# The first expert's rows picked on TensorE, and a reordered router, in a hybrid encoder layer

## The chip, the cores and the metric

The kernel runs on one core of one Trainium2 chip. The metric is the device time of one execution in microseconds (us), less is better. Engines are named as the profile does: PE (TensorE), DVE (VectorE), ACT (ScalarE), POOL (GpSimd) and SP, which here only issues transfers.

## What is computed

One layer on 512 tokens of 1024 channels, all fp32: a mixer (a state-space group and an attention group beside each other, then an output projection), LayerNorm, a mixture of 16 experts in 4 groups, LayerNorm. The part at issue is the router and the way into the first expert:

```python
h = _layer_norm(ALPHA * h + mix, ln1_g, ln1_b)
g_logits = hf @ rg_w + rg_b                       # 4 groups
g_val, g_idx = lax.top_k(jax.nn.softmax(g_logits, axis=-1), 1)
e_logits = ...                                    # the 4 experts of the chosen group
e_val, e_idx = lax.top_k(jax.nn.softmax(e_logits, axis=-1), TOP_K)   # TOP_K = 2
e_val = e_val / jnp.sum(e_val, axis=-1, keepdims=True)
weights = g_val[:, None] * e_val
...
for e in range(N_EXPERTS):
    act = jax.nn.silu(hf @ w_gate[e]) * (hf @ w_up[e])
    out = out + combine[:, e:e + 1] * (act @ w_down[e])
h = _layer_norm(ALPHA * h + out, ln2_g, ln2_b)
```

## The kernel before

The 512 tokens are four tiles of 128, `hh[0]` to `hh[3]`, 128 tokens on the partitions by 1024 channels. A product that has to be close to fp32 is made as three products of split operands (a high part and a low part of each).

*Output projection.* A tile has two halves of 512 columns; the second pass over a half is 4 blocks of k with 3 products each (`pw`, L810). DVE adds the sum to `hh` (L816) and takes the half's statistics (L1289).

*LayerNorm 1, for each tile:* `norm_stats` (mean and variance; the power -1/2 on POOL, `rs`, L142 and L143), `norm_gain` on DVE (L1171), `norm_bias`: ACT scales by `rs` (L1177), POOL adds the bias (L1178). `norm_store` writes the tile to `hb` in DRAM (from which experts gather rows) and to `ub` (to which they add their results).

*Router.* `u_T` transposes `hh` before gain and norm (`phT`, L1195, ACT copies it to `hT`); `logits` is eight fp32 products for each tile (`plg`, L1200); DVE applies norm and bias to the 20 logits (`lg`, L1203). `choose` ranks them by comparisons (`d`, L1239 to L1242) and makes `og`, the chosen group, and `mskb`, the chosen experts, as 0/1 (L1243, L1244; both write into tiles that the trace calls `arena` and `mskb`). `seat` counts with ten products of 0/1 matrices the seat of each token within its expert (`ppos`, `place`, L1254). For an expert, `seats_of` makes four matrices `se` of 128 tokens by 128 seats (L937), and `list_of` multiplies them with `entry` (token number in two parts, weight in three parts) to the list of token numbers `ix` and weights `wc` (`plist`, L945). `gather` then reads the listed rows from `hb` (L958). `weigh` works out the weights of the two experts on DVE and writes them into `entry` (L1261 to L1283), with two exponentials on ACT.

*Experts.* `xg_T` transposes the gathered rows (`pxg`, L980) and splits them into `xgh` (ACT) and `xgl` (DVE); `gate_up` makes the products of gate and up (`pg`, `pu`, L1004 to L1006), `down` those back to 1024 channels. `wsplit` makes the high and low part of a piece of weights, `eh` on ACT and `el` on DVE (L987, L988). Pieces of weights (`raw`, 512 KB each) stream in on SP's queue, 30 of them ahead of the experts.

The order on PE is the program's order throughout. Within the router block the code stands under a manual schedule, so the order on DVE, ACT and POOL is the program's too. Before, expert 0's list is made first, its rows are gathered from DRAM, expert 1's list and gather follow, then `weigh`, the weights' parts of the two lists (`plist` with three columns), the count `pcnt` of tokens per expert, and then the transpositions and the first gate product.

## Time and profile before

| | us |
|---|---|
| median of 3 runs | 645.06 (644.91 to 646.80) |
| profiled execution | 646.35 |
| span of the profiled execution | 644.3 |
| PE busy in it | 577.7 (90%) |
| DVE busy | 529.4 (82%) |
| ACT busy | 415.0 (64%) |
| POOL busy | 252.7 (39%) |

The times inside the trace count from the start of the span, which is the profiled execution's own, 1.29 us above the median in time. Busy shares are means over stages that have different limits: projections, scan and attention up to some 285 us, the last output projections and the router up to some 322 us, the experts up to some 610 us, then the end. The stage that the change touches is the second of these.

### The profile page before, as it was taken

To read this page: it belongs to the slowest core of one execution; us is meant where nothing else is said; L and a number is where in the kernel's file an instruction comes from. 1 tells how busy PE (TensorE), PEld (TensorE's weight loads), DVE (VectorE), ACT (ScalarE), POOL (GpSimd) and SP (SyncE) were. 2 spreads that over 40 slices of the span, in tenths; PEclk is the share of its full clock that TensorE was granted. 3 is DMA by queue.
4 is the path that set the end of the run, shared out by engine and by line. 5 is a ranking of instruction groups with operands and counts; after the bars stand their busy time and mean duration, and the time that the engine had idled before them with its cause. 6 is when DMAs were issued, how large, how long until landed. Compare 5 with 4: busy or idle time off the path is not lost.

```text
span 644.3 us, 9107 instructions
## 1 busy us (share of the span) xinstructions
PE 577.7 (90%) x3007; PEld 476.5 (74%) x3007; DVE 529.4 (82%) x869; ACT 415.0 (64%) x629; POOL 252.7 (39%) x256
## 2 busy tenths in 40 slices
PE   6788996999999989999389999999999999999950
PEld 4577786988777758788278888888888888877830
DVE  4986789688668797675879999999999999999672
ACT  5444353543578775333277888888888888887670
POOL 6537623833453541026423322333333332211282
PEclk9997996999999999998599999999999999999985
DMA  7421222221222175985879999999999999991442
GB/s 267 136 72 58 65 66 66 83 65 52 80 67 65 34 243 193 388 338 187 318 282 307 322 373 358 373 358 356 344 340 358 361 351 353 336 340 45 126 168 84
DMA packets 61702, 141.39 MB, mean 219 GB/s; under 512 B 9987, under 2 KB 10003, under 8 KB 61648
## 3 DMA queue, kind: packets, MB, share of 16 engines
q1 hardware_dynamic: 55168, 125.79, 55.0%
q0 software_dynamic: 5904, 12.85, 7.1%
q10 hardware_dynamic: 576, 2.10, 0.8%
q8 instruction: 25, 0.41, 0.3%
q14 instruction: 29, 0.24, 0.1%
HBM read 134.69 MB, written 14.68 MB: 232 GB/s over the span
## 4 chain that ended last, share of the span: by engine, by line
PE 57%; DVE 15%; ACT 8%; DMA 7%; issue 6%; POOL 5%; SPq 0%; POOLq 0%; ACTq 0%; DVEq 0%
PE pw L810 6%; PE pg L1004 5%; PE pg L1006 4%; PE pg L1005 4%; PE py L1038 4%; PE pu L1004 4%; PE pu L1006 4%; PE pu L1005 4%; PE py L1040 4%; PE py L1039 4%; PE pjT L250 3%; DVE acc L437 3%; DMA wr<-in_wu 2%; PE pxg L980 2%; POOL wl L234 1%
## 5 line engine op out<-in xcount | busy, mean ns | idle before, releaser
L987 ACT ACTIVATE eh<-wf 128x1024 fp32r<-128x1024 f32 x192 | 203.1, 1061 | 49.8 <-PE pg L1006 15.0
L234 POOL TENSOR_TENSOR wl<-wr,wh 128x512 fp32r<-128x512 f32 x40 | 56.8, 1441 | 43.5 <-ACT wh L229 40.7
L958 POOL DMA_INDIRECT xg<-hb,ix x16 | 21.0, 1315 | 113.1 <-PE pg L1006 107.9
L1044 POOL DMA_INDIRECT ub<-yo,ix x15 | 27.4, 1829 | 88.5 <-ACT at L103 54.4
L1038 PE MATMUL py<-eh,at 128*128 128x512 f32 x128 | 52.4, 410 | 2.7 <-ACT at L103 2.5
L1004 PE MATMUL pg<-eh,xgh 128*128 128x512 f32 x128 | 53.1, 415 | 0.8 <-ACT xgh L103 0.8
L1040 PE MATMUL py<-eh,at 128*128 128x512 f32 x128 | 50.9, 398 | 0.0
L1006 PE MATMUL pg<-eh,xgl 128*128 128x512 f32 x128 | 50.7, 396 | 0.0
L1004 PE MATMUL pu<-eh,xgh 128*128 128x512 f32 x128 | 50.0, 391 | 0.0
L1006 PE MATMUL pu<-eh,xgl 128*128 128x512 f32 x128 | 49.9, 390 | 0.0
L274 PE MATMUL pjR<-wh,xh 128*128 128x256 f32 x128 | 39.8, 311 | 8.9 <-ACT acc L429 7.5
L250 PE MATMUL pjT<-xh,wh 128*128 128x512 f32 x112 | 46.3, 413 | 1.2 <-DVE kl L674 1.2
L250 PE MATMUL pjT<-xh,wl 128*128 128x512 f32 x112 | 44.1, 394 | 0.0
L250 PE MATMUL pjT<-xl,wh 128*128 128x512 f32 x112 | 44.0, 393 | 0.0
L937 POOL TENSOR_SCALAR se<-seats,place 128x128 bf16<-128x128 f32 x56 | 43.4, 790 | 0.5
L274 PE MATMUL pjR<-wl,xh 128*128 128x256 f32 x128 | 38.3, 299 | 0.0
L274 PE MATMUL pjR<-wh,xl 128*128 128x256 f32 x128 | 38.1, 298 | 0.0
L274 PEld LDWEIGHTS pjR<-wh,xh 128*128 128x128 f32 x128 | 26.9, 210 | 9.6 <-ACT acc L429 7.9
L1038 PEld LDWEIGHTS py<-eh,at 128*128 128x128 f32 x128 | 24.5, 191 | 8.5 <-ACT at L103 2.7
L1040 PEld LDWEIGHTS py<-eh,at 128*128 128x128 f32 x128 | 24.4, 191 | 5.9 <-DVE at L104 0.8
L1006 PEld LDWEIGHTS pg<-eh,xgl 128*128 128x128 f32 x128 | 24.3, 190 | 6.0 <-DVE xgl L104 0.7
L1004 PEld LDWEIGHTS pg<-eh,xgh 128*128 128x128 f32 x128 | 24.3, 190 | 5.0 <-ACT xgh L103 1.2
(952 smaller groups left out, 1759.6 us busy)
## 6 DMA issues: line engine op xcount, KB each, us to landing
wf<-in_w_up SPq DMA_DIRECT2D x64, 512.0 KB, 11.6
wf<-in_w_gate SPq DMA_DIRECT2D x64, 512.0 KB, 11.7
wf<-in_w_down SPq DMA_DIRECT2D x60, 512.0 KB, 12.2
wr<-in_wu SPq DMA_DIRECT2D x22, 512.0 KB, 3.9
wor<-in_w_out SPq DMA_DIRECT2D x8, 512.0 KB, 3.3
hh<-in_x SPq DMA_DIRECT2D x4, 512.0 KB, 5.2
wf<-in_w_down POOLq DMA_DIRECT2D x4, 512.0 KB, 7.3
u<-ub SPq DMA_DIRECT2D x4, 512.0 KB, 6.0
```

The source lines that it names most:

```text
L234: G.tensor_tensor(l_[:, j], wr_[:, j], h_[:, j].bitcast(F32), op=OP.subtract)
L250: T.matmul(pt, lhsT=w_[:, k % 4, m * P:(m + 1) * P], rhs=x_[k], start=(i == 0), stop=(i == 23))
L274: T.matmul(pt, lhsT=x_[k][:, t * P:(t + 1) * P], rhs=w_[:, k % 4, :], start=(i == 0), stop=(i == 23))
L810: T.matmul(pw, lhsT=m_[k][:, ts_], rhs=wo[k][w_][:, c_], start=(i == 0), stop=(i == 11))
L937: eng.tensor_scalar(r[t], seats, place_(t), None, op0=OP.is_equal)
L987: A.activation(h_, src, AF.Copy)
L1004: T.matmul(pt, lhsT=h_[:, k], rhs=wh_[:, f], start=(k == 0), stop=False)
L1005: T.matmul(pt, lhsT=h_[:, k], rhs=wl_[:, f], start=False, stop=False)
L1006: T.matmul(pt, lhsT=l_[:, k], rhs=wh_[:, f], start=False, stop=(k == KC - 1))
L1038: T.matmul(pt, lhsT=h_[:, f], rhs=wh_[:, c_], start=(f == 0), stop=False)
L1040: T.matmul(pt, lhsT=l_[:, f], rhs=wh_[:, c_], start=False, stop=(f == 3))
L1044: G.indirect_dma_start(out=ub, out_offset=bass.IndirectOffsetOnAxis(ap=ix, axis=0), in_=yo, in_offset=None, bounds_check=S - 1, oob_is_err ...
```

## The change

Tiles 0 and 1 are chosen and seated while tile 2 is still projected (`choose(0, 2)`, `seat(0, 2)`), tiles 2 and 3 behind the logits. The rows of expert 0 are no longer gathered from DRAM and transposed: for each tile DVE makes a 0/1 matrix `pick[t]` (token by seat, in the memory of expert 0's `xg` tile), and PE multiplies `hh[t]`, 128 channels at a time, with it, summed over the four tiles. What results, `px`, is already transposed (channel by seat). A product of zeros opens each of its two banks; 32 products of 128x128 fp32 follow, the eight of tile 0 ahead of `seat(2, 4)`. `weigh` is cut in two by a `yield`, its first half ahead of the split of `px`, its second half behind it; then comes expert 0's list as a whole, then expert 1's weights and the count. Tile 2's bias is done by DVE in one operation (`NBV`), all stores go by POOL's queue, expert 1's matrices are made on POOL, and `og` is made with an added factor of ones.

```diff
-NBV = ()
+NBV = (2,)
-NXG = 26
+NXG = 25
-        se = seats_of(lp, lambda t: place[:, t, e:e + 1], V if e < 2 else G)
+        se = seats_of(lp, lambda t: place[:, t, e:e + 1], G)
...
-        V.tensor_scalar(c["og"], c["rank"][:, :, 0], 0.0, None, op0=OP.is_equal)
+        V.scalar_tensor_tensor(c["og"], c["rank"][:, :, 0], 0.0, onesf[:, None].to_broadcast([P, n, 4]), op0=OP.is_equal,
+                               op1=OP.mult)
...
+        for t in range(t0, t1):
+            pick[t] = xgs[0][:, t * P:(t + 1) * P]
+            V.scalar_tensor_tensor(pick[t], seats, place[:, t, 0:1], onesf.to_broadcast([P, P]), op0=OP.is_equal, op1=OP.mult)
+
+    def picked(ts, ks):
+
+        for k in ks:
+            if k % 4 == 0 and len(px) == k // 4:
+                px.append(bank("pj", "px"))
+
+                T.matmul(px[-1], lhsT=identb, rhs=maskq[:, 0:1].to_broadcast([P, 512]), start=True, stop=False)
+            for t in ts:
+                T.matmul(px[k // 4][:, k % 4 * P:(k % 4 + 1) * P], lhsT=hh[t][:, k * P:(k + 1) * P], rhs=pick[t],
+                         start=False, stop=(t == NT - 1 and k % 4 == 3))
...
                 if t == 2:
                     logits(1)
+                    choose(0, 2)
+                    next(ph_)
+                    next(ph_)
+                    next(ph_)
+                    seat(0, 2)
                 drop(ph_)
...
-        logits(2, range(4))
+        logits(2, range(3))
+        u_T(3, 1)
         logits(3, range(4))
         norm_stats(3)
-        norm_store(2, hb, A)
-        u_T(3, 1)
+        norm_store(2, hb, G)
         norm_gain(3)
...
         norm_shift(3)
...
+        norm_bias(3)
         logits(3, range(4, 8))
...
-        choose(2, 4)
-        seat()
-        call(0, False)
...
-        call(1, False)
-        load_pieces(NPRE, NPRE + GATED, G)
-        weigh()
-        for e in range(2):
-            lists[e][1] = list_of(lp, lists[e][1], entry_of(e), tokens=False)[1]
-        for i in range(2, 4):
-            dsp[0, i] = wsplit(raw[0, i])
+        logits(2, range(3, 8))
+        choose(2, 4)
+        picked((0,), range(KC))
+        seat(2, 4)
+        norm_store(3, hb, G)
+        picked((1,), range(KC))
+        picked((2, 3), range(4))
+        dsp[0, 2] = wsplit(raw[0, 2])
+        wg_ = weigh()
+        next(wg_)
+        xt_ = [wide("x", n, NX).rearrange("p (k s) -> p k s", s=P) for n in ("xgh", "xgl")]
+        for hf in range(2):
+            if hf:
+                picked((2, 3), range(4, 8))
+            split(*(t_[:, hf * 4:hf * 4 + 4] for t_ in xt_), px[hf].rearrange("p (k s) -> p k s", s=P))
+        call(1, False)
+        for t in range(2, 4):
+            norm_store(t, ub, G)
+        load_pieces(NPRE, NPRE + GATED, G)
+        dsp[0, 3] = wsplit(raw[0, 3])
+        drop(wg_)
+        lists[0] = list_of(lp, seats_of(lp, lambda t: place[:, t, 0:1], V), entry_of(0))
+        lists[1][1] = list_of(lp, lists[1][1], entry_of(1), tokens=False)[1]
-    xt_ = xg_T(xgs[0])
```

*First place: PE, from the last logits to the seats and from there to the first gate.* In the kernel before, the logits of tile 2 and of tile 3 are followed by the seat products, and the end of the stretch is the count (`pcnt`, a product of 0/1 matrices), the transpositions of the gathered rows (`pxg`) and the gate:

```order
L1358 LDWEIGHTS onesb
L1358 MATMUL pcnt<-mskb,onesb 128x16
L980 MATMUL pxg<-identf,xg_3007 128x128 x8
L1004 MATMUL pg<-eh,xgh 128x512
L1005 MATMUL pg<-el__3041,xgh 128x512
L1006 MATMUL pg<-eh,xgl 128x512
```

In the changed kernel the picks of tile 0 (`px`, with `hh` as the operand held in PE, and `xg_3005`, the memory of the 0/1 matrices, as the other) stand between the logits and the seat products:

```order
L1195 MATMUL plg_3019<-gw,hT 128x20 x3
L1190 MATMUL phT<-identf,hh 128x128 x4
L1195 MATMUL plg_3020<-gw,hT 128x20 x8
L1195 MATMUL plg_3019<-gw,hT 128x20 x5
L1264 LDWEIGHTS identb
L1264 MATMUL px<-maskq,identb 128x512
L1266 MATMUL px<-xg_3005,hh 128x128 x4
```

(the last three rows come once more, for the second bank) and the other 24 stand between the seat products (`ppos`) and the lists (`plist`, `se` the 0/1 matrices of an expert):

```order
L1251 MATMUL ppos<-mskb,onesb 128x16
L1252 LDWEIGHTS strictb
L1252 MATMUL ppos<-mskb,strictb 128x16
L1266 MATMUL px<-xg_3005,hh 128x128 x24
L940 LDWEIGHTS se
L940 MATMUL plist<-entry,se 128x2
```

and the gate follows the count directly:

```order
L1379 LDWEIGHTS onesb
L1379 MATMUL pcnt<-mskb,onesb 128x16
L999 MATMUL pg<-eh,xgh 128x512
L1000 MATMUL pg<-el__3041,xgh 128x512
L1001 MATMUL pg<-eh,xgl 128x512
```

The eight transpositions have gone from the place ahead of the gate; 32 products and two products of zeros have come, 24 of the products between the seats and the lists.

*Second place: DVE, behind the choice of tiles 2 and 3 (`mskb`).* In the kernel before, the place of each token (`place`) is followed by expert 0's matrices and list:

```order
L1243 TENSOR_SCALAR arena_3292<-arena_3292 128x8
L1244 SCALAR_TENSOR_TENSOR mskb<-arena_3292 128x32
L1254 SCALAR_TENSOR_TENSOR place<-ppos,mskb 128x64
L937 TENSOR_SCALAR se<-seats,place 128x128 x4
L950 TENSOR_REDUCE if__3336<-plist 128x1
L951 TENSOR_SCALAR ix<-if__3336 128x1
```

In the changed kernel by two picks, a low half of weights (`el`), the first half of `weigh`, and the split of `px`:

```order
L1253 SCALAR_TENSOR_TENSOR place<-ppos,mskb 128x32
L1256 SCALAR_TENSOR_TENSOR xg_3005<-seats,place,onesf 128x128 x2
L983 TENSOR_TENSOR el__3357<-wf,eh 128x1024
L1274 TENSOR_REDUCE arena_3180<-lg_3021 128x20
L1275 TENSOR_TENSOR lg_3021<-lg_3021,arena_3180 128x80
L1279 SCALAR_TENSOR_TENSOR arena_3360<-arena_3180 128x64
L1282 TENSOR_TENSOR arena_3360<-arena_3360,lg_3021 128x64
L1284 TENSOR_REDUCE arena_3180<-arena_3360 128x4
L1279 SCALAR_TENSOR_TENSOR arena_3180<-arena_3180 128x64
L99 TENSOR_TENSOR xgl<-px,xgh 128x512 x2
L945 TENSOR_REDUCE if__3394<-plist 128x1
L946 TENSOR_SCALAR ix<-if__3394 128x1
```

The split of the rows has moved ahead of the second half of `weigh`, and expert 0's matrices (L937, now L932) have left this place.

*Third place: DVE, at the end of the router.* In the kernel before, the last weights (`entry`) are followed by the weights' lists and by the low halves:

```order
L1283 TENSOR_TENSOR arena_3292<-arena_3292,entry 128x64
L1281 CAST entry<-arena_3292 128x64
L954 TENSOR_REDUCE wc<-plist 128x1 x2
L988 TENSOR_TENSOR el__3399<-wf,eh 128x1024
L988 TENSOR_TENSOR el__3403<-wf,eh 128x1024
L1359 TENSOR_REDUCE cnt_i<-pcnt 128x1
```

In the changed kernel by expert 0's four matrices and its whole list:

```order
L1297 TENSOR_TENSOR arena_3180<-arena_3180,entry 128x64
L1295 CAST entry<-arena_3180 128x64
L932 TENSOR_SCALAR se<-seats,place 128x128 x4
L945 TENSOR_REDUCE if__3433<-plist 128x1
L946 TENSOR_SCALAR ix<-if__3433 128x1
L949 TENSOR_REDUCE wc<-plist 128x1 x2
L1380 TENSOR_REDUCE cnt_i<-pcnt 128x1
```

The matrices and the list of expert 0 stand between the last of `entry` and the count, where there were only the weights' lists.

## Rows read from the trace of the kernel before

**Rows 1.** Busy time by stretch; columns: stretch, its us, PE, PEld, DVE, ACT, POOL, PEclk, DMA, GB/s

```profile
313.50:321.78 8.28, 2.48 (x22) 2.07 (x22) 6.86 (x26) 2.91 (x5) 5.70 (x8) 0.50 0.88 289
337.00:480.00 143.00, 142.69 (x700) 117.32 (x701) 137.10 (x169) 119.01 (x143) 50.19 (x50) 1.00 0.99 347
```

**Rows 2.** Chain of waits over the router; columns: start us, us, what

```profile
313.55 6.39 DMA xg<-hb,ix
...
319.98 1.97 PE pxg L980 x8
```

**Rows 3.** Timeline of PE; columns: start us, us, engine, line, operation, [idle before <-releaser]

```profile
292.24 1.05 PE L810 MATMUL pw<-woh,m 128*128 128x512 f32 x2
...
300.84 1.89 PE L1200 MATMUL plg<-gw,hT 128*128 128x20 f32 x16
...
304.63 1.89 PE L1200 MATMUL plg<-gw,hT 128*128 128x20 f32 x8 [0.62 <-ACT hT L1196]
...
318.86 0.25 PE L1358 MATMUL pcnt<-mskb,onesb 128*128 128x16 bf16 x4
...
321.78 0.80 PE L1004 MATMUL pg<-eh,xgh 128*128 128x512 f32 x1
...
324.51 0.45 PE L1004 MATMUL pu<-eh,xgh 128*128 128x512 f32 x1
```

**Rows 4.** Timeline of DVE, router

```profile
289.69 0.24 DVE L1203 SCALAR_TENSOR_TENSOR lg<-plg,rs,sh 128x20 f32<-128x20 f32 x1 [0.20 <-PE plg L1200]
...
303.25 1.39 DVE L1171 SCALAR_TENSOR_TENSOR hh<-hh,mv,l1g 128x1024 f32<-128x1024 f32 x1 [0.36 <-PE phT L1195]
...
305.80 0.33 DVE L1241 TENSOR_TENSOR d<-d,ahead 128x160 f32<-128x160 f32 x1
...
306.52 2.17 DVE L1243 TENSOR_SCALAR arena<-arena 128x8 f32<-128x8 f32 x1
...
308.83 0.23 DVE L1203 SCALAR_TENSOR_TENSOR lg<-plg,rs,sh 128x20 f32<-128x20 f32 x1
...
310.17 0.17 DVE L1243 TENSOR_SCALAR arena<-arena 128x8 f32<-128x8 f32 x1
310.37 0.19 DVE L1244 SCALAR_TENSOR_TENSOR mskb<-arena 128x32 bf16<-128x32 f32 x1
...
311.19 0.87 DVE L937 TENSOR_SCALAR se<-seats,place 128x128 bf16<-128x128 f32 x4
...
314.02 0.23 DVE L1261 TENSOR_REDUCE arena<-lg 128x20 f32<-128x80 f32 x1
...
315.22 0.16 DVE L1273 TENSOR_REDUCE arena<-arena 128x4 f32<-128x16 f32 x1
...
318.34 0.26 DVE L1281 CAST entry<-arena 128x64 bf16<-128x64 f32 x1
...
319.11 1.30 DVE L988 TENSOR_TENSOR el__3399<-wf,eh 128x1024 fp32r<-128x1024 f32 x1
...
322.62 0.69 DVE L104 TENSOR_TENSOR xgl<-pxg,xgh 128x512 fp32r<-128x512 f32 x1 [0.16 <-ACT xgh L103]
```

**Rows 5.** Timeline of PE, late in the program

```profile
609.32 2.05 PE L1114 MATMUL pl<-l2in,identf 16*128 16x128 f32 x16
```

**Rows 6.** Timeline of POOL, router

```profile
290.81 2.36 POOL L1178 TENSOR_TENSOR hh<-hh,l1b 128x1024 f32<-128x1024 f32 x1 [2.83 <-ACT hh L1177]
...
303.52 1.54 POOL L143 TENSOR_TENSOR rs<-rs,mhalf 128x1 f32<-128x1 f32 x1
306.32 2.34 POOL L1178 TENSOR_TENSOR hh<-hh,l1b 128x1024 f32<-128x1024 f32 x1 [1.26 <-ACT hh L1177]
```

**Rows 7.** Timeline of POOL, early in the program

```profile
43.15 6.32 POOL L234 TENSOR_TENSOR wl<-wr,wh 128x512 fp32r<-128x512 f32 x4 [12.51 <-ACT wh L229]
```

**Rows 8.** Timeline of DVE, in the same stretch

```profile
45.31 1.23 DVE L438 TENSOR_TENSOR acc<-acc,lack 128x3 f32<-128x3 f32 x1
```

**Rows 9.** Timeline of ACT, router

```profile
321.98 0.60 ACT L103 ACTIVATE xgh<-pxg 128x512 fp32r<-128x512 f32 x1 [0.26 <-PE pxg L980]
```

More of the change, by code (lines that the diff above doesn't have):

```diff
@@ L48 @@
 EARLY = 3
-NBV = ()
-NBO = 0
-CHO = 1
-UB = "AA"
+NBV = (2,)
 PT = ("o", "s")
 RY = 1.0
-HBE = 1
-UBE = 1
-NXG = 26
+NXG = 25
 WH_P = (0, 1)
@@ L1242, in choose, with seat @@
         V.tensor_reduce(rows_(c["rank"]), d, axis=AX.X, op=OP.add)
-        V.tensor_scalar(c["og"], c["rank"][:, :, 0], 0.0, None, op0=OP.is_equal)
+        V.scalar_tensor_tensor(c["og"], c["rank"][:, :, 0], 0.0, onesf[:, None].to_broadcast([P, n, 4]), op0=OP.is_equal,
+                               op1=OP.mult)
         V.scalar_tensor_tensor(mskb[:, t0:t1].rearrange("p t (g e) -> p t g e", e=4), c["rank"][:, :, 1:5], 2.0,
                                c["og"][:, :, :, None].to_broadcast([P, n, 4, 4]), op0=OP.is_lt, op1=OP.mult)
-    def seat():
+    pick, px = {}, []
+    def seat(t0, t1):
         pp_ = bank("s", "ppos")[:, :64].rearrange("p (t e) -> p t e", e=16)
-        for t in range(NT):
+        for t in range(t0, t1):
             for tt in range(t):
@@ L1253, in seat @@
             T.matmul(pp_[:, t], lhsT=strictb, rhs=mskb[:, t], start=(t == 0), stop=True)
-        V.scalar_tensor_tensor(place, pp_, 1.0, mskb, op0=OP.add, op1=OP.mult)
+        V.scalar_tensor_tensor(place[:, t0:t1], pp_[:, t0:t1], 1.0, mskb[:, t0:t1], op0=OP.add, op1=OP.mult)
+        for t in range(t0, t1):
+            pick[t] = xgs[0][:, t * P:(t + 1) * P]
[8 more added lines that the diff above has]
+                         start=False, stop=(t == NT - 1 and k % 4 == 3))
     def weigh():
@@ L1272, in weigh @@
                 A.activation(r1, r1, AF.Exp)
+        yield
         V.tensor_reduce(gs, gx, axis=AX.X, op=OP.add)
@@ L1292, in hybrid_layer @@
         for t in range(NT):
-            drop(proj_half(t, 0))
+            ph_ = proj_half(t, 0)
+            if t == 3:
+                next(ph_)
+                next(ph_)
+                u_T(2, 0)
+                u_T(2, 1)
+                norm_gain(2)
+            drop(ph_)
             if t in DSP0:
@@ L1297, in hybrid_layer @@
                 norm_shift(t - 1)
-                u_T(t - 1, 0)
-                u_T(t - 1, 1)
-                norm_gain(t - 1)
+                if t < 3:
+                    u_T(t - 1, 0)
+                    u_T(t - 1, 1)
+                    norm_gain(t - 1)
                 norm_bias(t - 1)
@@ L1305, in hybrid_layer @@
                     logits(1)
+                    choose(0, 2)
+                    next(ph_)
+                    next(ph_)
+                    next(ph_)
+                    seat(0, 2)
                 drop(ph_)
@@ L1309, in hybrid_layer @@
                     logits(0)
-                if t == 2 and CHO == 0:
-                    choose(0, 2)
                 if t:
-                    norm_store(t - 1, hb, (A, G)[HBE])
-                    norm_store(t - 1, ub, (A, G)[UBE])
+                    norm_store(t - 1, hb, G)
+                    norm_store(t - 1, ub, G)
         next(ph_)
@@ L1318, in hybrid_layer @@
         drop(ph_)
[L1319 removed]
+        logits(2, range(3))
+        u_T(3, 1)
         logits(3, range(4))
         norm_stats(3)
[L1322 to L1323 removed]
+        norm_store(2, hb, G)
         norm_gain(3)
[L1325 to L1327 removed]
         norm_shift(3)
[L1329 to L1356 removed]
+        norm_bias(3)
+        logits(3, range(4, 8))
+        logits(2, range(3, 8))
[14 more added lines that the diff above has]
+        call(1, False)
+        for t in range(2, 4):
+            norm_store(t, ub, G)
+        load_pieces(NPRE, NPRE + GATED, G)
+        dsp[0, 3] = wsplit(raw[0, 3])
+        drop(wg_)
+        lists[0] = list_of(lp, seats_of(lp, lambda t: place[:, t, 0:1], V), entry_of(0))
+        lists[1][1] = list_of(lp, lists[1][1], entry_of(1), tokens=False)[1]
+    pn = bank("s", "pcnt")[:, :16]
     for tt in range(NT):
@@ L1367, in hybrid_layer @@
         if e < NEXP - 2:
-            gu = gate_up(e, xt_)
+            gu = gate_up(e, xt_, "pj" if e else "o")
             for _ in range(EARLY):
```

18 lines of the change are left out of this document (removed).

## The prediction, made before the changed kernel had run

> **What bounds the kernel now.** Read first is the busy time by stretch [rows 1]. From 337 to 480 us, where the experts run, PE is busy 142.69 of 143.00 us at a granted clock of 1.00 (2.4 GHz): nothing there is to be had by shortening a wait. From 313.50 to 321.78 it is busy 2.48 of 8.28 us, at 0.50 (1.2 GHz). So the router, between the last row product of the output projection and the first gate product of expert 0 (321.78, [rows 3]), is a hole in PE's work, and what the change does to the time is what it does to the start of that product. The experts behind it move as one block: the same products follow in the same order, and PE has no slack to give or take.
>
> Second comes the chain of waits over the hole [rows 2]. Its largest piece is the gather of expert 0's rows, 6.39 us from 313.55; then the eight transpositions, 1.97 us, and the gate. What the chain does not show stands in DVE's list [rows 4]: while the gather flies, DVE works out the weights of the chosen experts (from 314.02 to 318.60) and makes two low halves of weights (from 319.11). The gather ends at 319.94, the weights' lists and the count at 319.1 (the `pcnt` row, 318.86 and 0.25). The gather thus hides the weighing nearly to the end. That is the question to ask of a change that takes the gather away: what is late next?
>
> **What goes.** For expert 0: the gather (6.39), its eight transpositions (1.97), and ahead of them the four 0/1 matrices and the list (seats and all, 3.0 us from `mskb`'s end at 310.56 to the gather at 313.55). Earlier choosing of tiles 0 and 1 also takes 1.73 us of DVE (`lg` to `mskb`, 308.83 to 310.56 where nothing stalls, [rows 4]) and the stall of 2.17 us in it out of tile 3's way. If nothing came in their place the gate could begin some 11 us sooner; all of it does get a substitute.
>
> **What comes, step by step, on the clock of the trace.**
>
> (a) *Tile 2.* The 0/1 choice of tiles 0 and 1 now follows `lg` at 289.69, and three seat products stand on PE after nine of the twelve products of tile 2's second half. The choice runs into POOL's bias add, 290.81 to 293.17 [rows 6]. The trace has the same pair: `og`, 8 elements wide, normally 0.17 us, took 2.17 us in 306.52 to 308.69 beside the add of 306.32 to 308.66 [rows 4, 6]. That the new `og` is an operation with two inputs is no way out: a two-input operation of 3 elements took 1.23 us beside POOL's subtractions [rows 7, 8]. So `mskb` comes at about 293.17 + 0.2 + 0.2 = 293.6, while the ninth product ends near 292.7 (the pair that begins at 292.24 is the ninth and tenth, two in 1.05, [rows 3]). PE and all behind it wait 1.0 us (bounds 0 and 2.0).
> The Trainium skill (SBUF — State Buffer, section SBUF: two separate sides) says that the port pair of the two engines is an exclusive lock for a whole instruction, which a DVE operation takes in a two-port mode or with two SBUF inputs; the 2.17 and 1.23 us agree with it. By it the rewritten `og` waits as the old one did, and the sum is the one given here; were it free of it, (a) would be 0 and the second stall in (c) nothing.
>
> (b) *Tile 3's norm.* `rs` ended at 303.52 + 1.54 = 305.06, held by DVE's gain of 303.25 to 304.64 [rows 4, 6]. The gain now waits for a transposition that stands 0.36 us earlier. With (a): 305.06 - 0.36 + 1.0 = 305.7.
>
> (c) *The choice of tiles 2 and 3.* After `rs` DVE does the shift, two `lg` and the comparisons; the second comparison would begin at about rs + 1.1 (0.74 in the trace, 305.80, plus two `lg` of under 0.2), POOL's add at rs + 1.26 (306.32), for 2.34. So `og` is caught, the comparison at the edge of it. With both caught, `mskb` is at rs + 1.26 + 2.34 + 0.3 + 0.35 + 0.2 + 0.2 = rs + 4.7 = 310.4; with none of it and without (a), at 304.7 + 2.4 = 307.1. Before it was 310.56. I take 310.4, since the trace shows this very collision.
>
> (d) *PE ahead of the seats.* From 302.0 on PE has 16 logit products, four transpositions, two zero products that open the banks, and the eight products of tile 0. The trace has two records for each fp32 product, so a logit product costs 1.89 / 8 = 0.24 at full clock, 1.89 / 4 = 0.47 at half clock (300.84 and 304.63, [rows 3]). At full clock it is through at 308.7, under the cover of (c); the ten seat products come right behind `mskb` and end at 310.7. Without (c)'s stall it would end at 307.6, just about with `mskb`.
>
> (e) *The remaining 24 products* of 128x128 fp32 by a 128x128 0/1 matrix. The trace has none; the nearest row has fp32 products of 128 columns, 2.05 / 8 = 0.25 us each at full clock, though with 16 partitions [rows 5]; the other bound is the half-clock 0.47. PE has by then stood some 2 us, and in the trace, after standing, it ran at half clock from 321.78 to 324.51, 2.7 us, before a product took 0.45 instead of 0.80 [rows 3]. At full clock throughout: 24 x 0.25 = 6.0, end 316.7. Restarting at half clock: 5.8 products in 2.7 us, 18.2 in 4.6, end 318.0. I take the middle, 317.3. Other DVE work (two picks, one low half of 1.3, the first half of the weighing, 1.2) fits under it.
> The Trainium skill (Perfetto Trace Analysis, section Transposes) asks for a transposition rather than an ordinary product where data are only moved. Here the eight transpositions took 1.97 us at half clock (0.25 each), the product at that clock 0.47, which agrees; and there are 32 products for 8 transpositions. By that rule the change should lose on PE, and the sum says so too.
>
> (f) *DVE's tail behind the last product.* Now nothing flies that could hide it. In its new order: ACT's high half 0.65 [rows 9] and DVE's low half 0.16 + 0.69; the list of expert 1, two operations, 0.35; a low half of weights 1.25; the second half of the weighing, 315.22 to 318.60, 3.38 less a wait, 3.25; four matrices 0.87; then lists, weights and count, 1.2, an estimate: from `entry`'s end at 318.60 to `pcnt`'s end at 319.11 it took 0.5 for two hand-overs between DVE and PE, and here there are four and three short operations [rows 3, 4]. Sum 8.4. The first gate stands behind the lists and the count in PE's order, so it starts at 317.3 + 8.4 = 325.7, against 321.78: +3.9 us.
>
> Edits that I cost at nothing: expert 1's matrices on POOL, which is idle from about 310 (needed only an expert later); the moved stores and the piece of weights that now waits for them (its reader is three experts on); one preload fewer ahead; gate banks "o" (their last readers, the logits, are long done). If the cover of expert 1's gather (expert 0's 48 gate and up products) were gone, it would cost its 6.39.
>
> **Sum.** The profiled execution took 646.35 us (span 644.3), 1.29 above the median of the three runs, 645.06. 646.35 + 3.9 = 650.3 on its clock, 649.0 against the median. A measurement of this kernel can tell about 0.3%, 1.9 us, from no change.
>
> **The rivals.**
> 1. *It comes out even.* No collision on DVE in (a) and (c), full clock: seats at 307.9, last product 313.9, gate 322.3, +0.5, 645.6 us. For it: the second `og` of the trace took 0.17; the two queues shift by tenths of a microsecond. Against: the add's start hangs on the same `rs` as the choice.
> 2. *Faster.* A product by a 0/1 matrix costs about what a transposition costs at full clock, half of 0.25. With 24 x 0.12 and no collision DVE's chain alone is left: 307.1 + 11.9 = 319.0, -2.8, 642.3 us. It decides where a product costs under about 0.15 and nothing collides. Against: the logit products, with a sixth of the columns, cost 0.24.
> 3. *Much slower.* PE never comes back to 2.4 GHz in the hole, as in the 8.28 us ahead of the gate in the trace [rows 1]: 24 x 0.47 = 11.3 behind 310.7, gate 330.4, +8.6, 653.7 us; with the logits at half clock too, 657.9.
>
> **How the numbers follow.** Main case (DVE's weighing is what is late next, +2 to +6 us): 0.58. Even: 0.23. Faster: 0.09. Much slower: 0.10. The likeliest gives 649.0. The range leaves out the faster case and most of the much slower one: 644.4 (the even case, 1.2 below its 645.6) to 654.5. The main case's own range is 647.0 to 651.5. Faster by over 0.3%: 0.09; within: 0.24; slower: 0.67.
>
> **What would show it.** Right: the chain of waits has no gather between `mskb` and the first gate; PE waits for DVE's `entry` or `se`, and the first gate begins near 325.7; the 24 `px` products take 6 to 7.5 us together; an `og` of about 2 us beside POOL's add. Wrong: a gate before 322, the last `px` product before 314, or a hole behind the first gate that was not there before, as expert 1's rows or a piece of weights arriving late would make.

## The result, and the profile after

The changed kernel takes 649.87 us in the median of 4 runs (649.08 to 650.59), against 645.6 us of the kernel before measured beside it (644.91 to 646.80): ratio 1.0071, interval 1.0055 to 1.0086. It is slower by 4.3 us, and the prediction had said 649.0, +3.9 on its own trace. The profiled execution took 650.47 us, span 648.5.

The busy time by stretch of the kernel after (columns as in [rows 1]: stretch, its us, PE, PEld, DVE, ACT, POOL, PEclk, DMA, GB/s) has the hole in another place:

```profile
302.40:312.00 9.60, 9.31 (x63) 8.93 (x61) 6.84 (x14) 3.23 (x4) 6.22 (x6) 0.69 0.86 307
312.00:318.00 6.00, 6.00 (x55) 5.92 (x52) 3.85 (x11) 1.03 (x4) 2.28 (x2) 0.93 0.59 203
318.00:325.40 7.40, 0.87 (x12) 0.59 (x11) 6.06 (x24) 1.53 (x2) 5.51 (x8) 0.84 0.43 157
325.40:330.10 4.70, 4.70 (x15) 3.71 (x16) 0.78 (x2) 1.06 (x1) 1.10 (x2) 0.52 1.01 384
```

From 302.40 to 318 PE is busy nearly throughout, with logits and picks, where before it stood. From 318 to 325.4 it is busy 0.87 of 7.40 us. In these 7.4 us the second half of the weighing is done and expert 0's matrices and list are made. Before, the weighing ran while the gather flew, and the matrices and the list stood ahead of the gather. Then the gate runs 4.7 us at a granted clock of 0.52.

The chain of waits names the pieces (start us, us, what):

```profile
292.17 2.18 DVE arena L1238
...
294.61 0.17 PE ppos L1252
...
307.62 0.43 PE px L1264
308.05 1.71 PE px L1266 x8
...
310.18 1.71 PE px L1266 x8
...
312.06 5.91 PE px L1266 x48
...
318.48 1.06 ACT eh L982
...
319.56 1.23 DVE el__3407 L983
...
322.04 0.56 DVE entry L1295
...
325.33 0.28 PE pcnt L1379 x4
325.61 0.63 PE pg L999
```

No gather and no transposition of gathered rows stands in it any more [rows 2]: it goes from `og` beside POOL's add (292.17) through the picks (`px`) to the two halves of a piece of weights (`eh` on ACT, 318.48, and `el` on DVE, 319.56), the weighing (`entry`, 322.04), the count (325.33), and the gate.

PE's timeline of the kernel after (as [rows 3]) shows the three waits of PE that the change made or moved, and the price of a pick:

```profile
294.61 0.17 PE L1252 MATMUL ppos<-mskb,strictb 128*128 128x16 bf16 x1 [1.62 <-DVE mskb L1240]
...
303.41 0.63 PE L1190 MATMUL phT<-identf,hh 128*128 128x128 f32 x4 [0.29 <-DVE hh L811]
...
311.91 6.04 PE L1266 MATMUL px<-xg,hh 128*128 128x128 f32 x48
...
324.11 0.82 PE L940 MATMUL plist<-entry,se 128*128 128x5 bf16 x8 [6.08 <-DVE se L932]
325.33 0.28 PE L1379 MATMUL pcnt<-mskb,onesb 128*128 128x16 bf16 x4 [0.40 <-DVE wc L949]
325.46 0.77 PE L999 MATMUL pg<-eh,xgh 128*128 128x512 f32 x1
```

The 24 picks behind the seats took 6.04 us with the last one's modelled end, 5.91 in the chain: 0.25 each, at a clock of 0.93 from 312 to 318. Then PE waited 6.08 us for `se` and 0.40 for the list's weights, and the first gate product began at 325.46.

DVE's timeline (as [rows 4]) has both stalls beside POOL's adds:

```profile
292.17 2.17 DVE L1238 SCALAR_TENSOR_TENSOR arena<-arena,onesf 128x8 f32<-128x8 f32 x1
...
307.93 1.91 DVE L1234 TENSOR_TENSOR d<-lg 128x160 f32<-128x160 f32 x1
309.88 0.33 DVE L1236 TENSOR_TENSOR d<-d,ahead 128x160 f32<-128x160 f32 x1
...
310.59 0.17 DVE L1238 SCALAR_TENSOR_TENSOR arena<-arena,onesf 128x8 f32<-128x8 f32 x1
310.79 0.30 DVE L1240 SCALAR_TENSOR_TENSOR mskb<-arena 128x32 bf16<-128x32 f32 x1
...
316.83 0.69 DVE L99 TENSOR_TENSOR xgl<-px,xgh 128x512 fp32r<-128x512 f32 x1 [1.44 <-ACT xgh L98]
318.62 0.69 DVE L99 TENSOR_TENSOR xgl<-px,xgh 128x512 fp32r<-128x512 f32 x1 [1.10 <-ACT xgh L98]
```

and POOL's (as [rows 6]) the adds:

```profile
291.95 2.35 POOL L1173 TENSOR_TENSOR hh<-hh,l1b 128x1024 f32<-128x1024 f32 x1 [1.72 <-ACT hh L1172]
...
307.32 2.35 POOL L1173 TENSOR_TENSOR hh<-hh,l1b 128x1024 f32<-128x1024 f32 x1 [0.73 <-ACT hh L1172]
```

The new `og` took 2.17 us, as the old one did; the two-input form is no way out. At the second place it was the first comparison that was caught (1.91 us), and `og` then ran in 0.17. The two idle times ahead of `xgl` (in the brackets: 1.44 and 1.10 us of DVE waiting for the picked rows) are the ones in which the first experiment puts the weighing.

**How the trace of the prediction stands among others of the same kernel.** Two more traces of the kernel before were taken later. The stages count here from the first transposition of tile 0 (`phT`), so that differences in the first stages fall out; each column is the start of one event, in us behind it. The last column is the measured time against before.

| kernel | last projection product | last seat product | first gate product | expert 1's transpositions | time |
|---|---|---|---|---|---|
| before, the trace of the prediction | 22.5 | 32.7 | 43.7 | 56.3 | |
| before, second trace | 21.0 | 31.1 | 41.9 | 54.4 | |
| before, third trace | 21.0 | 31.1 | 41.4 | 54.5 | |
| after | 22.9 | 32.7 | 46.3 | 59.6 | +0.71% |
| e1, weighing early | 23.0 | 32.0 | 42.5 | 56.3 | +0.33% |
| e2, gate first | 23.0 | 33.0 | 38.7 | 53.2 | -0.29% |
| e3, reorder alone | 23.1 | 31.9 | 41.4 | 54.7 | +0.27% |
| e4, bias on DVE | 22.0 | 30.1 | 43.5 | 56.8 | +0.50% |
| e5, before with filling | 21.0 | 31.1 | 41.7 | 54.5 | -0.02% |
| e6, before with stores on POOL | 21.0 | 31.2 | 41.2 | 55.6 | +0.33% |
| e7, gather, gate first | 23.0 | 31.8 | 40.7 | 54.1 | +0.05% |
| e8, after with filling | 22.9 | 32.0 | 45.1 | 56.4 | +0.67% |
| v1, gate first, weighing early | 23.0 | 32.1 | 37.7 | 50.2 | -0.58% |
| v2, the same, bias on DVE | 22.0 | 29.6 | 35.2 | 48.8 | -0.78% |

The trace of the prediction ran the projection of tile 2 partly at half clock (the pair at 292.24 in 1.05 us, [rows 3], where the second trace has 0.63 for such a pair), which the other two did not, and it lost 1.5 us there. Its gather, at 6.39 us, was the longest of the three: PE waited 0.87, 0.52 and 0 us for it behind the count. Against the two other traces the gate of the changed kernel is 4.4 to 4.9 us late, and expert 1 some 5.1. From tile 0's transposition to the end of the span the trace of after is 5.2 us longer than those two (369.3 against 364.1): what is late at expert 1 is late at the end.

### The profile page after: what moved, and what is told of

Read it like the earlier page. It is cut to its first block, busy times and chain, and to the rows that moved or that the text cites. A ratio compares the mean times of both kernels' runs of the same rounds, so it can differ in the third digit from the quotient of the medians.

```text
span 648.5 us, 9222 instructions
## 1 busy us (share of the span) xinstructions
PE 584.4 (90%) x3061; PEld 482.8 (74%) x3061; DVE 532.4 (82%) x871; ACT 414.1 (64%) x628; POOL 256.4 (40%) x262
## 4 chain that ended last, share of the span: by engine, by line
PE 61%; DVE 14%; ACT 8%; issue 6%; DMA 5%; POOL 4%; SPq 0%; POOLq 0%; ACTq 0%; DVEq 0%
PE pw L805 6%; PE pg L999 5%; PE pg L1001 4%; PE pu L999 4%; PE pg L1000 4%; PE py L1033 4%; PE pu L1001 4%; PE pu L1000 4%; PE py L1035 4%; PE py L1034 4%; PE pjT L245 3%; PE pjR L269 3%; DVE acc L432 3%; PE pxg L975 2%; DMA wr<-in_wu 2%
## 5 line engine op out<-in xcount | busy, mean ns | idle before, releaser
L229 POOL TENSOR_TENSOR wl<-wr,wh 128x512 fp32r<-128x512 f32 x40 | 56.8, 1444 | 43.4 <-ACT wh L224 40.6
L932 POOL TENSOR_SCALAR se<-seats,place 128x128 bf16<-128x128 f32 x60 | 47.1, 794 | 1.2 <-DVE place L1253 0.6
L245 PE MATMUL pjT<-xh,wh 128*128 128x512 f32 x112 | 46.3, 414 | 1.3 <-DVE kl L669 1.3
L999 PEld LDWEIGHTS pu<-eh,xgh 128*128 128x128 f32 x128 | 24.3, 190 | 5.2
```

The source lines that it names most:

```text
L229: G.tensor_tensor(l_[:, j], wr_[:, j], h_[:, j].bitcast(F32), op=OP.subtract)
L245: T.matmul(pt, lhsT=w_[:, k % 4, m * P:(m + 1) * P], rhs=x_[k], start=(i == 0), stop=(i == 23))
L932: eng.tensor_scalar(r[t], seats, place_(t), None, op0=OP.is_equal)
L999: T.matmul(pt, lhsT=h_[:, k], rhs=wh_[:, f], start=(k == 0), stop=False)
```

## The experiments

My theory was that DVE's tail (weighing, matrices, list: 7.5 us between the last pick and the gate) is what is late, because lists and count stand ahead of the gate in PE's order. The rivals: that the price is PE's own 34 added products, or DVE's stalls beside POOL's adds. All times are against the kernel before, run beside each on the same chip.

**e1: the weighing in one piece, ahead of the split.**

```diff
                 A.activation(r1, r1, AF.Exp)
-        yield
...
-        wg_ = weigh()
-        next(wg_)
+        weigh()
...
-        drop(wg_)
```

> The changed kernel with one edit: the weighing is not cut in two, its second half (3.1 us on DVE) stands ahead of the split of the picked rows, where DVE idles 1.44 and 1.10 us for PE. Theory (DVE's tail between the last picked product and the first gate is what is late): the weighing ends near 318.5, the two low halves of the rows follow, the gate begins near 323.1 in place of 325.46, the time is 0.3% to 0.4% under the changed kernel's (about +0.35% against before). Rival (PE's own added products are the price, the DVE tail is covered): no change from the changed kernel, +0.7% against before. Rival (the stalls of DVE beside POOL's adds are the price): no change either.

Measured: 647.89 us, ratio 1.0033 (1.0020 to 1.0045). On PE:

```profile
320.09 0.88 PE L940 MATMUL plist<-entry,se 128*128 128x5 bf16 x8 [3.29 <-DVE se L932]
321.37 0.28 PE L1376 MATMUL pcnt<-mskb,onesb 128*128 128x16 bf16 x4 [0.40 <-DVE wc L949]
321.50 0.77 PE L999 MATMUL pg<-eh,xgh 128*128 128x512 f32 x1
```

The wait of PE for `se` fell from 6.08 to 3.29 us. The gate began 42.5 us behind tile 0's transposition in place of 46.3. Of these 3.8 us, 2.8 are the wait; the rest is that in this trace the seats came 0.7 sooner and the picks took a little less, as PE ran partly at full clock ahead of them. The gate came earlier than forecast (321.50 for 323.1); the theory's time came out, +0.33% for +0.35%, where both rivals had said no change.

**e2: the gate first.** All gate and up products of expert 0 stand ahead of the lists and the count on PE, half of them ahead of the weighing's second half on DVE.

```diff
         dsp[0, 3] = wsplit(raw[0, 3])
+        gu0 = gate_up(0, xt_, "o")
+        next(gu0)
+        next(gu0)
         drop(wg_)
+        next(gu0)
+        next(gu0)
...
-            gu = gate_up(e, xt_, "pj" if e else "o")
-            for _ in range(EARLY):
+            gu = gate_up(e, xt_) if e else gu0
+            for _ in range(EARLY if e else 0):
```

> The changed kernel with the 48 gate and up products of expert 0 ahead of its lists and the count in PE's order, 24 of them ahead of the second half of the weighing in DVE's order. Theory (the gate waits for DVE's tail only because lists and count stand ahead of it): first gate product near 318.2, then DVE's low halves for pieces 4 to 7 pace PE by some 2 us; the transpositions for expert 1, at 338.8 in the changed kernel and 334.4 before, begin near 331 to 332, so the time is 0.3% to 0.5% under before. Rival (the picked products on PE are the price): the gate moves, but the time stays within 0.2% of the changed kernel, +0.5% to +0.7% against before.

Measured: 643.51 us, ratio 0.9971 (0.9959 to 0.9984): faster than both kernels. On PE:

```profile
317.48 0.47 PE L999 MATMUL pg<-eh,xgh 128*128 128x512 f32 x1
...
324.53 0.50 PE L1000 MATMUL pg<-el__3449,xgh 128*128 128x512 f32 x1 [1.11 <-DVE el__3449 L983]
...
331.73 0.26 PE L1384 MATMUL pcnt<-mskb,onesb 128*128 128x16 bf16 x4 [1.50 <-DVE wc L949]
...
331.95 1.07 PE L975 MATMUL pxg<-identf,xg 128*128 128x128 f32 x8
```

The gate began at 317.48, right behind the picks and without a wait. Then DVE's low halves paced it (1.11 us at 324.53), and the count waited 1.50 for the list's weights. Expert 1's transpositions came where the theory had them (331.95, forecast 331 to 332). The same picks on PE, the same 0/1 matrices, no work taken away: the order alone turned +0.71% into -0.29%. The rival that the products are the price falls with that.

**e3: the reorder alone.** Expert 0's rows are gathered and transposed as before, both experts' matrices are made on DVE, and weighing and lists stand in the order of before; choices, norms and stores stay as changed.

```diff
...
-        picked((0,), range(KC))
         seat(2, 4)
         norm_store(3, hb, G)
-        picked((1,), range(KC))
...
+        call(0, False, V)
+        call(1, False, V)
...
+        drop(weigh())
+        for e in range(2):
+            lists[e][1] = list_of(lp, lists[e][1], entry_of(e), tokens=False)[1]
...
+    xt_ = xg_T(xgs[0])
```

> The changed kernel without its picks: choices, norms, stores and expert 1's queue as changed, but expert 0's rows gathered from memory and transposed as before, both experts' matrices on DVE, the weighing and the lists in the order of before. Theory (the picks and the order around them cost the 0.7%, the reorder nothing): within 0.3% of before. Rival (the reorder of choices and norms costs it: the wait of 1.62 us on PE in tile 2): +0.4% to +0.7% against before.

Measured: 647.06 us, ratio 1.0027 (1.0016 to 1.0038). The reorder as a whole gains nothing: the choice of tiles 0 and 1 no longer stands in tile 3's way, but PE's wait in tile 2 (23.1 against 21.0 in the table) makes up for it, and the last seat comes 0.8 us later than in the two other traces of before, not earlier. The gate is not late all the same (41.4): the gather took 4.5 us here, less than in any trace of before. The time was inside the bound that the theory set, though not at zero.

**e4: no add of POOL beside the choices.**

```diff
-NBV = (2,)
+NBV = (1, 2, 3)
```

> The changed kernel with the bias of tiles 1, 2 and 3 done by DVE (only tile 2 in the changed kernel), so that no add of POOL stands beside the two choices. Both 0/1 choices then run without a stall (0.17 in place of 2.17 us, 0.32 in place of 1.91), DVE has two operations of 1.28 us more. My theory: PE's wait for the first seats falls from 1.62 to about 0.4, everything behind comes 1.2 us sooner, +0.5% against before. Rival (the stalls are the whole price): -0.1% to +0.1% against before. Rival (they are covered by PE): no change, +0.7%.

Measured: 648.71 us, ratio 1.0050 (1.0030 to 1.0069). On DVE, a bias and the two choices behind it:

```profile
291.51 1.28 DVE L1170 SCALAR_TENSOR_TENSOR hh<-hh,rs,l1b 128x1024 f32<-128x1024 f32 x1
...
292.98 0.32 DVE L1234 TENSOR_TENSOR d<-lg 128x160 f32<-128x160 f32 x1
...
294.05 0.17 DVE L1238 SCALAR_TENSOR_TENSOR arena<-arena,onesf 128x8 f32<-128x8 f32 x1
...
307.92 0.33 DVE L1234 TENSOR_TENSOR d<-lg 128x160 f32<-128x160 f32 x1
...
309.04 0.17 DVE L1238 SCALAR_TENSOR_TENSOR arena<-arena,onesf 128x8 f32<-128x8 f32 x1
```

The comparisons and `og` run in 0.32 and 0.17 us, and PE's wait for the first seats fell from 1.62 to 0.66. The time came out as forecast, 0.2% under the changed kernel by the medians, though the two intervals overlap. In the trace the gate came 2.8 us sooner, and not by the stalls alone: 1.0 of it is PE's wait, and PE also ran longer at full clock ahead of the seats (26 records of logits in 3.04 us, 3.74 in after). The stalls are not the whole price: +0.50% is left.

**e5: the kernel before with its hole filled.** Twenty products by zeros into a bank that nobody reads.

```diff
         load_pieces(NPRE, NPRE + GATED, G)
+        wz_ = bank("t", "warm")
+        for _ in range(20):
+            T.matmul(wz_, lhsT=identb, rhs=maskq[:, 0:1].to_broadcast([P, 512]), start=True, stop=True)
         weigh()
```

> The kernel before with one thing added: 20 products by zeros (128x512, bf16) on PE in its hole behind the two lists of token numbers (313.7 to 318.6 of the trace of before), into a bank that nobody reads. Theory (after an idle stretch PE starts at 1.2 GHz, and that is part of what the hole costs): the eight transpositions take about 1.0 in place of 1.97 us and the first six gate products 0.23 in place of 0.43 each, so the experts begin 2.2 us sooner, -0.3% against before. Rival (the granted clock does not hang on such products, or the gather alone sets the time): no change.

Measured: 645.92 us, ratio 0.9998 (0.9987 to 1.0010): a miss. On PE:

```profile
319.49 1.07 PE L980 MATMUL pxg<-identf,xg 128*128 128x128 f32 x8
320.81 0.50 PE L1004 MATMUL pg<-eh,xgh 128*128 128x512 f32 x1 [0.25 <-ACT xgh L103]
...
322.74 0.50 PE L1006 MATMUL pg<-eh,xgl 128*128 128x512 f32 x1 [1.20 <-DVE xgl L104]
```

The mechanism is there: the eight transpositions took 1.07 in place of 1.97 us. But the gate product that needs the low half of the rows then waited 1.20 us for DVE, which was making two low halves of weights first (`el`, from 319.11 in [rows 4]). And the filling had itself made DVE late, as DVE's timeline shows:

```profile
319.45 0.27 DVE L954 TENSOR_REDUCE wc<-plist 128x1 f32<-128x3 f32 x2 [1.32 <-PE plist L945]
```

The products by zeros still ran when the last of `entry` was written (318.14), so the weights' lists began at 319.18, 1.30 us behind the start of that operation, where they stand 0.30 behind it in the trace of the prediction (318.64 on PE, behind the operation of 318.34 in [rows 4]). DVE waited 1.32 us for them, and its low halves came that much later. What the clock gave, these waits took: expert 1's transpositions stand at 54.5, as in the two other traces of before. A shorter filling was not tried, so this run does not say what the clock alone is worth.

**e6: the stores alone.** The kernel before with its last stores on POOL's queue.

```diff
-UB = "AA"
+UB = "GG"
...
-        norm_store(2, hb, A)
+        norm_store(2, hb, G)
...
-        norm_store(3, hb, A)
+        norm_store(3, hb, G)
```

> The kernel before with the stores of tiles 2 and 3 (to hb and ub) issued on POOL's queue, as the changed kernel has them, in place of ACT's. Two things are asked. In the router: ACT loses 0.3 to 1.3 us of issuing, the gather of expert 0 is behind one more issue on POOL; I expect -0.1% to +0.2%. At the start of the program: the changed kernel and each variant of it so far began its second stage (19.33 us in before) 0.7 to 1.3 us later, while nothing there was edited. If the queue that the stores use has to do with that, this kernel starts late too (about +0.2%); if it is spread between executions, it does not.

Measured: 647.77 us, ratio 1.0033 (1.0020 to 1.0047), more than I had expected. In its trace the gate was not late (41.2), but it ran at half clock longer:

```profile
318.90:326.30 7.40, 7.06 (x28) 5.27 (x26) 4.69 (x8) 2.25 (x3) 3.07 (x3) 0.50 0.96 355
```

0.50 for 7.4 us, to the twelfth gate product, where the trace of the prediction had six such products. Expert 1's transpositions came 1.1 us later than in the two other traces of before. From tile 0's transposition to the end of the span this trace is 1.7 us longer than those two, so most of the measured 0.33% is in it, and none of it ahead of the gate. Why the queue of the stores does this is open. So e3's 0.27% may well be the stores and not the choices; which of the two was not told apart. The changed kernel has its stores on this queue too, and it was not run with them on ACT's. In its trace 4.4 to 4.9 of the 5.2 us were lost by the first gate product, where e6 had lost nothing, so the stores explain little of it if they act there as they do in e6.

**e7: the gather, with the gate first.** e3 with the order of the best kernel: the gate and up products of expert 0 ahead of the weights' lists and the count. The main lines, against e3:

```diff
...
-        for e in range(2):
-            lists[e][1] = list_of(lp, lists[e][1], entry_of(e), tokens=False)[1]
+        xt_ = xg_T(xgs[0])
         for i in range(2, 4):
             dsp[0, i] = wsplit(raw[0, i])
+        gu0 = gate_up(0, xt_, "pj")
+        for _ in range(3):
+            next(gu0)
+        for i in range(6, 8):
+            dsp[0, i] = wsplit(raw[0, i])
+        for e in range(2):
+            lists[e][1] = list_of(lp, lists[e][1], entry_of(e), tokens=False)[1]
+        next(gu0)
...
-    xt_ = xg_T(xgs[0])
...
```

> The reorder alone (expert 0's rows gathered and transposed, no picks), and the gate and up products of expert 0 ahead of the weights' lists and the count, as in the best kernel so far. Theory (picks are worth having once nothing stands behind them: with them the gate begins at 318.1 in the trace's clock, with the gather not before the transpositions are through at some 320 to 321): within 0.3% of before, and 0.4% to 0.8% slower than the best kernel with picks. Rival (the order did it all, the picks give nothing): -0.5% or better against before.

Measured: 645.39 us, ratio 1.0005 (0.9993 to 1.0017). On PE:

```profile
317.69 1.97 PE L975 MATMUL pxg<-identf,xg 128*128 128x128 f32 x8 [4.25 <-DMA xg<-hb,ix]
319.49 0.79 PE L999 MATMUL pg<-eh,xgh 128*128 128x512 f32 x1
```

PE stood 4.25 us for the gather, which took 4.1 us here (issued at 313.53), and then did its transpositions at half clock, 1.97 us. With the gather the order brings the time back to that of before, 0.2% under e3, and no further; with the picks it goes on. Between this kernel and v1, below, lie 0.6%.

**e8: the changed kernel with its hole filled.** As e5, with 24 products, behind expert 1's list of token numbers.

```diff
         call(1, False)
+        wz_ = bank("t", "warm")
+        for _ in range(24):
+            T.matmul(wz_, lhsT=identb, rhs=maskq[:, 0:1].to_broadcast([P, 512]), start=True, stop=True)
         for t in range(2, 4):
             norm_store(t, ub, G)
```

> The changed kernel with 24 products by zeros (128x512, bf16) on PE in its hole between the picks and expert 0's list (318.0 to 324.1). In the kernel before such a filling brought the granted clock back to 1.00 ahead of the transpositions, but the gate then waited 1.20 us for DVE. Here the gate's operands are ready long before. Theory: the first ten gate products take 0.23 in place of 0.43, 2 us less, 0.3% under the changed kernel, +0.35% to +0.4% against before. Rival (the restart at half clock is covered, DVE paces expert 0): +0.6% to +0.7%.

Measured: 649.33 us, ratio 1.0067 (1.0052 to 1.0083). In the profiled execution the filling did what was expected:

```profile
316.00:323.80 7.80, 6.51 (x42) 3.08 (x43) 6.06 (x24) 1.54 (x2) 5.54 (x8) 1.00 0.45 153
323.80:328.50 4.70, 4.70 (x25) 3.88 (x24) 1.95 (x3) 2.37 (x3) 1.07 (x2) 1.00 1.01 382
```

The granted clock is 1.00 where it was 0.84 and 0.52 in the changed kernel, and from the first gate product to expert 1's transpositions it took 11.3 us in place of 13.3. But that execution was the shortest of the six (648.08), 1.25 us under their median, and the profiled execution of after was 0.6 above its own. The median is only 0.5 us under the changed kernel's, less than the interval can tell from nothing. The forecast failed by its number, and why the 2 us of the trace do not show in the median stays open.

**v1: gate first and weighing early.** The two orders of e1 and e2 together: the weighing cut in three, its second part in DVE's first idle time ahead of the split, its third part in the second; expert 0's matrices on POOL; the gate and up products behind the picks; expert 0's list behind the 36th of the 48.

```diff
         V.tensor_tensor(oh0, oh0, oh1, op=OP.add)
+        yield
...
         next(wg_)
+        next(wg_)
+        call(1, False)
+        se0 = seats_of(lp, lambda t: place[:, t, 0:1], G)
...
             if hf:
+                drop(wg_)
                 picked((2, 3), range(4, 8))
...
-        call(1, False)
...
-        drop(wg_)
-        lists[0] = list_of(lp, seats_of(lp, lambda t: place[:, t, 0:1], V), entry_of(0))
+        gu0 = gate_up(0, xt_, "o")
+        for _ in range(3):
+            next(gu0)
+        for i in range(6, 8):
+            dsp[0, i] = wsplit(raw[0, i])
+        lists[0] = list_of(lp, se0, entry_of(0))
         lists[1][1] = list_of(lp, lists[1][1], entry_of(1), tokens=False)[1]
+        next(gu0)
...
```

> The changed kernel put together from the first two experiments: the weighing's second half in DVE's idle time around the split of the picked rows, all gate and up products of expert 0 ahead of the count, its lists behind the 36th of 48, its 0/1 matrices on POOL. Theory: PE goes from the picks into the gate without waiting for DVE, the transpositions for expert 1 begin near 330 (331.95 in the kernel with the gate first alone), -0.5% against before. Rival (DVE's low halves of the weights pace expert 0 whatever stands between): no better than -0.3%.

Measured: 642.55 us, ratio 0.9942 (0.9929 to 0.9955), a little better than forecast; expert 1's transpositions began at 330.20.

**v2: the same with the bias of tiles 1 to 3 on DVE.** Against v1:

```diff
-NBV = (2,)
+NBV = (1, 2, 3)
```

> The same with the bias of tiles 1, 2 and 3 on DVE. In the changed kernel that gave 0.2%, by a shorter wait of PE in tile 2. Theory: it adds up, -0.65% to -0.7% against before. Rival (with the tail gone DVE is the bound, and its 2.6 us more are paid): no better than the kernel without it.

Measured: 641.33 us, ratio 0.9922 (0.9902 to 0.9943), the best median of all, 4.7 us under the kernel before. Its interval overlaps that of v1, so the step from v1 is likely and not shown. By stretch:

```profile
302.40:312.00 9.60, 8.70 (x80) 8.54 (x81) 8.43 (x20) 1.87 (x3) 5.79 (x7) 1.00 1.02 338
312.00:330.00 18.00, 16.59 (x107) 13.63 (x106) 14.86 (x39) 12.25 (x17) 13.16 (x14) 1.00 0.65 211
```

From 312 to 330 PE is busy 16.59 of 18.00 us at a clock of 1.00; the kernel after has two stretches at 0.84 and 0.52 there. The hole is gone, and with it the restart at half clock. On PE the first gate product:

```profile
315.16 0.48 PE L999 MATMUL pg<-eh,xgh 128*128 128x512 f32 x1
```

315.16 is 35.2 us behind tile 0's transposition, where after has 46.3.

**The kernel before, two more traces.**

> The kernel before, unedited, for a second trace. Asked: whether its second stage begins at 19.33 us again, or some 1 us later as in all ten other traces (then the difference at the start is spread between executions, and not the change's); and whether the gather of expert 0 takes 6.39 us again or about 5, as the kernels e3 and e6 let one suppose.

> The kernel before, unedited, for a third trace, with the same questions.

Measured: 645.25 and 644.29 us. Their second stages began 0.56 and 0.60 us later than in the trace of the prediction, those of the changed kernel and of all others 0.7 to 1.5 us (e5, which starts and stores as before does, 0.95). At tile 0's transposition the second trace of before stands at 279.27, behind the changed kernel's 279.21. So the 1.1 us by which the changed kernel's profiled execution was late there are within what the kernel before shows between executions. PE's wait for the gather in the second of the three traces:

```profile
318.54 0.25 PE L1358 MATMUL pcnt<-mskb,onesb 128*128 128x16 bf16 x4
319.32 1.97 PE L980 MATMUL pxg<-identf,xg 128*128 128x128 f32 x8 [0.52 <-DMA xg<-hb,ix]
321.12 0.79 PE L1004 MATMUL pg<-eh,xgh 128*128 128x512 f32 x1
```

In the third there is none: the transpositions follow the count at once. In the kernel before, gather and weighing end within some 0.9 us of each other.

## Why the prediction came out right

The time (649.0 forecast, 649.87 measured), the sign and the mechanism held: DVE's weighing became what is late, the forecast's main case at 0.58. The steps are set here against the trace of after. Its tile 0 began 1.14 us later than in the trace of the prediction (`phT` at 279.21 against 278.07), ahead of the router and within the spread just shown; so "on the forecast's clock" below means the time of the trace of after less 1.14.

- (a) *Tile 2.* The mechanism was right (`og` 2.17 us beside the add), the term too small: PE waited 1.62 us, not 1.0. I had read the end of the ninth product off the half-clock stretch that the two other traces of before don't have. Against those the last projection product came 1.9 us late (22.9 against 21.0).
- (b) *Norm of tile 3.* `rs` forecast for 305.7; DVE's next operation, which waits for it, began at 306.08, 304.9 on the forecast's clock. The forecast's trace had carried 1.5 us of half-clock projection into this step, which the trace of after did not pay.
- (c) *Second choice.* `mskb` forecast for 310.4, ended at 311.09, 309.95 on the forecast's clock. The collision was there, with another operation in it: the first comparison for 1.91 us, not the second and `og`.
- (d) *PE ahead of the seats.* The step that was wrong in kind. PE was to be through with tile 0's picks at 308.7, under the cover of (c); on the forecast's clock it was through at 310.5, and it, not `mskb`, released the seats. The picks ran at 0.43 us each (1.71 for four, 308.05 and 310.18 in the chain), the half-clock price of the forecast's slower rival. The forecast took the full clock there and gave no reason for it; PE's granted clock in 302.40 to 312 was 0.69. In finer stretches it was 1.00 up to 305.40, 0.50 from 306.40 to 312.40 and 1.00 again from 313.00, with PE at work on logits and picks nearly without a gap. What it cost was small, since (c) was nearly as late: the last seat stood at 310.7, where the forecast had its end.
- (e) *The 24 picks.* 5.91 us, 0.25 each, the value from [rows 5]; the forecast's middle was 6.6. The restart at half clock, on which the middle rested, did not come: PE, being late, had not stood, and only the first of these picks were still at half clock. That PE's not having stood is the reason is an inference.
- (f) *The tail.* 7.5 us (317.97 to 325.46), forecast 8.4: too large by 0.9. Lists and operations overlap with their neighbours' ends more than the single durations say: the weighing's second half took 2.95 us to the start of `se`, forecast 3.25, and lists, weights and count 0.88, forecast 1.2. ACT's high half was put at 0.65, where [rows 9] has 0.60.
- *What was put at nothing or was not in the sum.* The moved stores were put at nothing; alone, on the kernel before, they cost 0.33% (e6), behind the gate. What they cost beside the picks was not measured. The gate's restart at half clock reached to 330.05, over ten products, where before six had been slow (321.78 to 324.51, [rows 3]). From the first gate product to expert 1's transpositions it took 13.3 us, against 12.5 to 13.1 in the three traces of before.

So the gate was forecast for 47.6 us behind tile 0's transposition and came at 46.3: (e) and (f) were 1.6 us too dear, and 0.2 us between the seats and the first of the 24 picks had been left out. And the gate before, from which the shift was counted, stood at 43.7 in the one trace that the forecast had and at 41.4 and 41.9 in the two others. The two errors cancelled in the difference, +3.9 forecast against 4.4 to 4.9 between traces and 4.3 in time. The likeliest case was named rightly; that its size came out within a microsecond owes something to chance.

Of the rivals, the even one needed DVE free of POOL's adds: e4 took the adds away and still was at +0.50%. (Its gate at 43.5 is about where that rival had it, 322.3 or 44.2; but the gate before, at 41.4 to 41.9 in the two other traces, is earlier than in the trace from which the rival was reckoned.) The faster one needed a pick for under 0.15 us; it cost 0.25. (Its sum adds 11.9 us to 307.1 without saying from which rows.) The much slower one came true in step (d) alone, and there DVE covered most of it.

The rule of the Trainium skill that was weighed in (e) (Perfetto Trace Analysis, section Transposes: transpose rather than multiply) agrees with the prices, 0.25 us for a pick at full clock against 1.07 / 8 = 0.13 for a transposition (e5). It does not decide the case: v2, with 32 picks for eight transpositions, is the fastest kernel here: what the picks replace is a gather of 4 to 6 us as well, for which PE stood 4.25 us in e7.

## What to carry to other kernels

Taking the longest piece out of a chain gains only as much as the next one is shorter, so list what ran beside it and ask where that goes: here the weighing had run under the gather for nothing, and stood in the open when the gather went. Then look at what the waiting instruction truly needs. The gate needed the picked rows alone, and waited for lists and a count only because they stood ahead of it in an in-order queue; moving them behind it turned +0.7% into -0.3%, with the weighing put into DVE's idle time and expert 0's matrices on POOL it became -0.6%, and -0.8% with the biases moved off POOL. And look at more than one trace where a step hangs on tenths of a microsecond.

## What the runs showed of the hardware

- An 8-element operation of DVE with two inputs took 2.17 us beside a POOL add of 2.35 us, as the one-input form had; once the adds were gone it took 0.17.
- The picks, fp32 products with 128 columns, cost 0.25 us at a granted clock near 1.00 and 0.43 at half clock. 13 of the logit products, of 20 columns, took 3.58 us ahead of them, 0.28 each. In that stretch PE was busy 9.31 of 9.60 us and had a clock of 0.69: there a busy PE was no sign of a full clock.
- Products by zeros in a hole kept the granted clock at 1.00 (e8) and halved the transpositions behind them (1.07 against 1.97 us in e5); in neither kernel did the median show it. In e5 they also ran 1.0 us into the next work.
- The same gather took 6.4, 6.0 and 5.6 us from issue to landing in the three traces of the kernel before, and 4.8 (e6), 4.5 (e3) and 4.1 (e7) in the three traces with the last stores on POOL's queue. In e6 that queue is the only edit, so the shorter gather goes with it, by one trace each; how the one acts on the other is not shown, and e6 was slower all the same.
